# When the decay matrices of the gated delta heads are made, and in which tiles

## The chip, the cores and the metric

One core of a Trainium2 chip. The metric is the device time of one execution in microseconds (us); runs of one kernel are compared by their median. TensorE (PE) does the matrix products, VectorE (DVE), ScalarE (ACT) and GpSimd (POOL) the elementwise work, and SyncE (SP) issues most of the DMAs. PE's granted clock is shown as a share of full speed: 1.00 is 2.4 GHz, 0.50 is 1.2 GHz.

## What is computed

One decoder layer over 1024 tokens of width 2048, in float32: a modulated input is projected by one large matrix, four retention heads and eight gated delta heads mix along the sequence, an output projection and a layer norm follow. The change is in the gated delta heads. For one head, with queries q, keys k, values v (1024 x 128 each), log decays g and step sizes beta, in chunks of C tokens (64 in the reference, 128 in the kernel; the result is the same function):

```
gcum  = cumsum(g within the chunk)
decay = exp(gcum_i - gcum_j) for i >= j, else 0
A     = strictly_lower((k * beta) @ k.T * decay)
T     = inverse(I + A)
attn  = lower(q @ k.T * decay)
per chunk, with the state S carried on:
  v_new = T @ (v*beta) - T @ (k*beta*exp(gcum)) @ S
  o     = (q * exp(gcum)) @ S + attn @ v_new
  S     = S * exp(g_last) + (k * exp(g_last - gcum)).T @ v_new
```

So `decay`, a 128 x 128 matrix per chunk and head, is used twice: for A, with the keys alone, and for attn, with the queries. exp(gcum) as a row over the chunk scales the queries.

## The kernel before

**Stages.** First the modulation and the first projection columns (to about 220 us of the span), then the main stage: for each of the eight gated delta heads four projections (K, V, Q and the gate GG) of 1024 tokens by 128 columns, then three retention heads' projections, then the output projection with the layer norm (from about 1585 us). A projection (`gemm_cm`, L476) is 96 matmuls of 512 columns, each operand split in a high and a low part.

**Order.** PE's instructions run in the order in which the program writes them. Between two matmuls of a projection, `tick` (L419) lets a generator go on by one step: first one of the list `aux`, then the first of `heads`, if its waiting time, counted in ticks, has run out. So the small matmuls of the heads are woven in between the large ones at fixed places, and a `yield n` says after how many ticks the next step may come. All other engines are ordered by the framework's planner: it estimates when the inputs and the tile buffer of an operation are ready, so that an operation can stand on its engine ahead of others that were written before it. Once planned, every engine works through its list in order.

**A head** has four generators, in this order: `gdn_keys` (L759: transposes of k, the squares for its norm, k k' times decay, then a forward substitution on DVE by way of two DMA round trips through DRAM), `gdn_values` (L883), `gdn_merge` (L831: block inverses joined on PE, L850 to L880, after transposes on DVE, L840) and `gdn_scan` (L895). The merge is due 210 ticks after the end of the key step. The scan takes two halves of four chunks; before them, for each half, it makes q k' (L907), multiplies it by the decay matrix into the tile `et` (L908), transposes q (L913), sums its squares on ACT (L745) and scales q on POOL (L917). Then, chunk by chunk, with four ticks between: L930 (k times state), w on DVE (L932), L936 (inverse times w), u on ACT (L938), L942 (state update; new state on DVE, L945 or L947), L951 and L952 (output). `gdn_out` follows by way of `aux`.

**The decay matrix.** `decay_prep` stores gcum of all chunks and heads in DRAM (`gc_d`, L718). `gate_rows` (L736) loads one half of a head, 4 chunks x 128, to all 128 partitions (256 KB) into a tile of the tag `gb` with two buffers; the tag is also used by `gdn_merge` (Tm) and by the loads of the modulation gate in the later stage (graw). `decay_matrix` (L751) adds the column term and the mask on DVE (four L755 of 128 x 128) and takes the exponential on ACT (L757, 128 x 512). `gdn_keys` does this in place in gb for both halves, `gdn_scan` does it again into et, takes the exponential of the row itself (L915) and multiplies q by it (L917). That makes four loads, 16 L755, four L757 and two L915 per head.

Of the kernel before, what the change touches and what calls it, by code (L numbers as in the profile page):

```python
# [7 lines left out]
F32 = mybir.dt.float32  # L8
F32R = mybir.dt.float32r
I32 = mybir.dt.int32  # L10
AF = mybir.ActivationFunctionType
ALU = mybir.AluOpType
# [3 lines left out]
P = 128  # L16
# [6 lines left out]
GH = 8  # L23
# [35 lines left out]
def hybrid_layer_kernel(ctx: ExitStack, tc: tile.TileContext, x, c, w_ada, b_ada, w_in, gdn_conv_w,  # L59
                        gdn_a_log, gdn_dt_bias, ret_gn_w, ret_gn_b, gdn_norm_w, w_out, ln_w, ln_b,  # L60
                        tab, out):
    nc = tc.nc
# [350 lines left out]
    def spawn(gen, wait=0.0):  # L413
        heads.append([gen, clock[0] + wait])
# [260 lines left out]
    def decay_prep(gab, dec):  # L675
        n = [P, NC, GH]
        ones_ = mp.tile([P, P], F32, name="ones_", tag="gb", bufs=2)
        V.memset(ones_, 1.0)
        tmpt = mp.tile([P, 4, NC, GH], F32, name="dtmp", tag="ktok")

        def tl(nm):
            return const.tile(n, F32, name=nm, tag=nm)
        alog = const.tile([P, GH], F32, name="alog")
        dtb = const.tile([P, GH], F32, name="dtb")
        nc.sync.dma_start(out=alog, in_=gdn_a_log.broadcast_to([P, GH]))
        nc.sync.dma_start(out=dtb, in_=gdn_dt_bias.broadcast_to([P, GH]))
        S.activation(out=alog, in_=alog, func=AF.Exp)
        ga, e, z, z2 = (tmpt[:, i] for i in range(4))
        g = tl("g_")
        V.tensor_tensor(out=ga, in0=gab[:, :, 0:8], in1=dtb[:, None, :].broadcast_to(n), op=ALU.add)  # L690
        V.scalar_tensor_tensor(out=e, in0=ga, scalar=-1.0, in1=ga, op0=ALU.mult, op1=ALU.max)
        S.activation(out=e, in_=e, func=AF.Exp, scale=-1.0)
        V.tensor_scalar(out=z, in0=e, scalar1=2.0, scalar2=None, op0=ALU.add)
        V.reciprocal(out=z, in_=z)
        V.tensor_tensor(out=z, in0=z, in1=e, op=ALU.mult)
        V.tensor_tensor(out=z2, in0=z, in1=z, op=ALU.mult)
        V.tensor_scalar(out=g, in0=z2, scalar1=1.0 / 15, scalar2=None, op0=ALU.mult)
        for d in (13, 11, 9, 7, 5, 3):
            V.scalar_tensor_tensor(out=g, in0=g, scalar=1.0 / d, in1=z2, op0=ALU.add, op1=ALU.mult)
        V.scalar_tensor_tensor(out=g, in0=g, scalar=1.0, in1=z, op0=ALU.add, op1=ALU.mult)  # L700
        V.tensor_scalar(out=ga, in0=ga, scalar1=0.0, scalar2=None, op0=ALU.max)
        V.scalar_tensor_tensor(out=g, in0=g, scalar=2.0, in1=ga, op0=ALU.mult, op1=ALU.add)
        V.scalar_tensor_tensor(out=g, in0=g, scalar=-1.0, in1=alog[:, None, :].broadcast_to(n),
                               op0=ALU.mult, op1=ALU.mult)
        beta = tl("beta")
        V.tensor_scalar(out=beta, in0=gab[:, :, 8:16], scalar1=-87.0, scalar2=None, op0=ALU.max)
        S.activation(out=beta, in_=beta, func=AF.Exp, scale=-1.0)
        V.tensor_scalar(out=beta, in0=beta, scalar1=1.0, scalar2=None, op0=ALU.add)
        V.reciprocal(out=beta, in_=beta)
        gf = g.rearrange("p c h -> p (c h)")  # L710
        yield 40
        pc = small_ps()
        PE.matmul(pc[:, 0:64], tri, gf, start=True, stop=True)
        PE.matmul(pc[:, 64:128], ones_, gf, start=True, stop=True)
        PE.matmul(pc[:64, 128:256], gf, tri, start=True, stop=True)
        gcT = mp.tile([64, P], F32, name="gcT", tag="et")
        S.copy(gcT, pc[:64, 128:256])
        nc.sync.dma_start(out=gc_d, in_=gcT)  # L718
        ngc, neg, ktl, egl = tl("ngc"), tl("neg"), tl("ktl"), tl("egl")
        pv = pc[:, 0:128].rearrange("p (a c h) -> p a c h", a=2, h=GH)  # L720
        V.tensor_scalar(out=ngc, in0=pv[:, 0], scalar1=-1.0, scalar2=None, op0=ALU.mult)
        S.activation(out=neg, in_=ngc, func=AF.Exp, scale=-1.0)
        V.tensor_scalar(out=neg, in0=neg, scalar1=-1.0, scalar2=None, op0=ALU.mult)
        S.activation(out=egl, in_=pv[:, 1], func=AF.Exp)
        V.tensor_tensor(out=ktl, in0=pv[:, 1], in1=ngc, op=ALU.add)
        S.activation(out=ktl, in_=ktl, func=AF.Exp)
        dec.update(beta=beta, ngc=ngc, neg=neg, ktl=ktl, egl=egl)
        yield 0

    B8 = [P, NC, P]  # L730
    B4 = [P, 4, P]

    def c4(t):
        return t.rearrange("p (c i) -> p c i", i=P)

    def gate_rows(h, hf):  # L736
        gb = mp.tile([P, 512], F32, name="gb", tag="gb", bufs=2)
        nc.sync.dma_start(out=c4(gb), in_=gc_d.rearrange("(c h) i -> h c i", h=GH)
                          [h:h + 1, 4 * hf:4 * hf + 4].broadcast_to(B4))
        return gb  # L740

    def sum_squares(src, dst):
        junk = gp.tile([P, P], F32, name="junk", tag="xt")
# [7 lines left out]
    def decay_matrix(h, hf, out, gb, dec):  # L751
        for j in range(4):
            ch = 4 * hf + j
            cl = slice(j * P, (j + 1) * P)
            V.scalar_tensor_tensor(out=out[:, cl], in0=gb[:, cl], scalar=dec["ngc"][:, ch, h:h + 1], in1=maske,  # L755
                                   op0=ALU.add, op1=ALU.add)
        S.activation(out=out, in_=out, func=AF.Exp)  # L757

    def gdn_keys(h, st, k, dec, Pm):  # L759
# [2 lines left out]
        nb = c4(sup[:, 1024:2048])  # L762
        kt_ = mp.tile(B8, F32, name="ktok", tag="ktok")
        ss = gp.tile([P, NC], F32, name="ssk", tag="ssk")
        ets = []
        for hf in range(2):
            gb = gate_rows(h, hf)
            decay_matrix(h, hf, gb, gb, dec)
            ets.append(c4(gb))
        for hf in range(2):  # L770
            pk = small_ps()
            for j in range(4):
# [16 lines left out]
        for hf in range(2):  # L789
            pkk = small_ps()  # L790
            for j in range(4):
                cl = slice((4 * hf + j) * P, (4 * hf + j + 1) * P)
                PE.matmul(pkk[:, j * P:(j + 1) * P], k[:, cl], k[:, cl], start=True, stop=True)  # L793
            for j in range(4):
                ch = 4 * hf + j
                V.scalar_tensor_tensor(out=nb[:, ch], in0=pkk[:, j * P:(j + 1) * P], scalar=nco[:, ch:ch + 1],
                                       in1=ets[hf][:, j], op0=ALU.mult, op1=ALU.mult)
            yield 2

        s1 = drs.tile([4, NC, 1024], F32, name="s1", tag="s1")  # L800
# [79 lines left out]
            V.tensor_copy(Pm[h0, c4s, h1], px2[h0, :, 0:64])  # L880
        yield 5

    def gdn_values(st, v):  # L883
        vs = mp.tile(B8, F32, name="vs", tag="vs")
        for hf in range(2):
            c4s = slice(4 * hf, 4 * hf + 4)
            pv = small_ps()
            for j in range(4):
                ch = 4 * hf + j
                PE.transpose(pv[:, j * P:(j + 1) * P], v[:, ch * P:(ch + 1) * P], ident)  # L890
            V.tensor_tensor(out=vs[:, c4s], in0=c4(pv), in1=st["sk"][:, c4s, None].broadcast_to(B4), op=ALU.mult)
            yield 3
        st["vs"] = vs

    def gdn_scan(h, st, k, q, dec, Pm):  # L895
        kt_, vs, co = st["kt"], st["vs"], st["co"]
        et = mp.tile(B8, F32, name="et", tag="et")
        ssq = gp.tile([P, NC], F32, name="ssq", tag="ssq")
        for hf in range(2):
            c4s = slice(4 * hf, 4 * hf + 4)  # L900
            gb = gate_rows(h, hf)
            ef = et[:, c4s].rearrange("p c i -> p (c i)")
            decay_matrix(h, hf, ef, gb, dec)
            pqk = small_ps()
            for j in range(4):
                cl = slice((4 * hf + j) * P, (4 * hf + j + 1) * P)
                PE.matmul(pqk[:, j * P:(j + 1) * P], k[:, cl], q[:, cl], start=True, stop=True)  # L907
            V.tensor_tensor(out=et[:, c4s], in0=c4(pqk), in1=et[:, c4s], op=ALU.mult)  # L908
            yield 2
            pq = small_ps()  # L910
            for j in range(4):
                ch = 4 * hf + j
                PE.transpose(pq[:, j * P:(j + 1) * P], q[:, ch * P:(ch + 1) * P], ident)  # L913
            sum_squares(pq, ssq[:, c4s])
            S.activation(out=gb, in_=gb, func=AF.Exp)  # L915
            hs = slice(hf * 512, (hf + 1) * 512)
            G.tensor_tensor(out=q[:, hs], in0=q[:, hs], in1=gb, op=ALU.mult)  # L917
            yield 2
        state = None
        for hf in range(2):  # L920
            o = mp.tile(B4, F32, name="og", tag="o", bufs=2)
# [81 lines left out]
    for h in range(GH):  # L1003
        k = conv_silu(gemm_cm(GK + h * P), 8 + h) if h else k_first
        st = {}
        spawn(gdn_keys(h, st, k, dec, Pm), CONV_WAIT if h else 0)
        v = conv_silu(gemm_cm(GV + h * P), 16 + h)
        spawn(gdn_values(st, v), 56)
        spawn(gdn_merge(st, Pm))
        q = conv_silu(gemm_cm(GQ + h * P), h)  # L1010
        spawn(gdn_scan(h, st, k, q, dec, Pm), 38)
        st["sg"] = silu_gate(gemm_cm(GG + h * P))
# [237 lines left out]
```

## Time and profile before

| what | value |
|---|---|
| median of 3 runs | 1962.99 us (1962.37 to 1963.16) |
| the profiled execution | 1964.96 us, its span 1963.20 us |
| PE busy | 1875.3 us, 96% of the span |
| DVE, ACT, POOL busy | 58%, 28%, 9% |
| mean granted clock | 0.988 |
| stage of the gated delta heads | about 220 to 1160 us of the span |

Busy time of PE is that of its matmuls; their ends are modelled, since matmuls overlap. In a row of the timeline the first number is the start in us of the span, the second the time from start to end of what the row merges, `x2` the number of instructions, and in brackets stands how long the engine was idle just before and what ended that. One product of 32-bit operands is two instructions in the small matmuls.

### The profile page before, as it was taken

The numbers are of one execution on the slowest core, as the hardware profiler recorded it, in microseconds if no ns is written. First come the engines' busy times: TensorE is split into PE (matmuls) and PEld (weight loads), VectorE is DVE, ScalarE is ACT, GpSimd is POOL, SyncE is SP. The second block draws the span as 40 slices with busy tenths as digits, with TensorE's granted clock in tenths as the row PEclk, the third lists the DMA queues.
The fourth block names the chain that finished last, engine by engine and source line by source line (L and its number), as shares of the span: only waits on it lengthen the run. The fifth ranks groups of instructions, "written<-read, shape, count | busy, mean of one in ns | idle before, by whom it ended". The sixth has DMA issues, their size and how long they took to land.

```text
span 1963.2 us, 27906 instructions
## 1 busy us (share of the span) xinstructions
PE 1875.3 (96%) x10336; PEld 1584.3 (81%) x10336; DVE 1143.9 (58%) x2833; ACT 555.0 (28%) x1243; POOL 170.4 (9%) x165
## 2 busy tenths in 40 slices
PE   4999999999999999999999999999999999998996
PEld 3788878787878788787878798898898878886885
DVE  6785666575746657574756642544542534458557
ACT  2543232323223231423223221211211232234221
POOL 0000111000000000100000000100100100005102
PEclk9999999999999999999999999999999999999998
DMA  9994223221222212221222241144141266345532
GB/s 293 324 305 133 72 50 84 49 72 45 77 51 73 54 55 67 54 73 49 68 56 72 65 124 49 49 140 134 44 129 48 65 202 227 124 135 185 180 115 89
DMA packets 249195, 210.07 MB, mean 107 GB/s; under 512 B 44425, under 2 KB 208858, under 8 KB 248290
## 3 DMA queue, kind: packets, MB, share of 16 engines
q1 hardware_dynamic: 246434, 199.89, 34.7%
q0 software_dynamic: 2624, 8.39, 1.2%
q8 instruction: 81, 1.33, 0.3%
q14 instruction: 56, 0.46, 0.1%
HBM read 189.31 MB, written 18.92 MB: 106 GB/s over the span
## 4 chain that ended last, share of the span: by engine, by line
PE 72%; DMA 6%; DVE 4%; issue 1%; POOL 1%; ACT 1%; SPq 0%; DVEq 0%; ACTq 0%; POOLq 0%
PE pg L476 44%; PE po L1105 14%; PE pg L508 6%; DMA gb<-gc_d 4%; DMA raw<-mixed 1%; DMA graw<-in_w_ada_dram 1%; PE ps L793 1%; POOL z L1161 1%; PE ps L936 1%; PE ps L930 1%; DVE et L755 1%; PE ps L952 1%; PE ps L603 1%; PE ps L951 1%; POOL yc L917 0%
## 5 line engine op out<-in xcount | busy, mean ns | idle before, releaser
L476 PE MATMUL pg<-h_hi,w_hi 128*128 128x512 f32 x1376 | 451.7, 400 | 0.0
L476 PE MATMUL pg<-h_hi,w_lo 128*128 128x512 f32 x1376 | 448.5, 399 | 0.0
L476 PE MATMUL pg<-h_lo,w_hi 128*128 128x512 f32 x1376 | 447.4, 399 | 0.0
L1105 PE MATMUL po<-wr,ms 128*128 128x512 f32 x1380 | 319.6, 393 | 8.4 <-DVE wr L1052 5.8
L1105 PEld LDWEIGHTS po<-wr,ms 128*128 128x128 f32 x1380 | 260.9, 190 | 65.4 <-DVE wr L1052 8.1
L94 ACT CAST w_hi<-w_raw 128x512 fp32r<-128x512 f32 (+1 forms) x203 | 126.1, 621 | 603.8 <-PE pg L476 455.3
L476 PEld LDWEIGHTS pg<-h_hi,w_hi 128*128 128x128 f32 x1376 | 256.4, 189 | 48.9 <-ACT w_hi L94 1.7
L476 PEld LDWEIGHTS pg<-h_lo,w_hi 128*128 128x128 f32 x1376 | 257.3, 189 | 47.6
L476 PEld LDWEIGHTS pg<-h_hi,w_lo 128*128 128x128 f32 x1376 | 256.7, 188 | 47.5 <-issue 0.2
L95 DVE TENSOR_TENSOR w_lo<-w_raw,w_hi 128x512 fp32r<-128x512 f32 (+1 forms) x203 | 144.6, 712 | 218.9 <-ACT w_hi L94 214.5
L1052 DVE TENSOR_TENSOR wr<-raw,wr 128x512 fp32r<-128x512 f32 x116 | 88.1, 762 | 109.9 <-ACT wr L1050 107.9
L508 PE MATMUL pg<-w_lo,h_hi 128*128 128x256 f32 (+1 forms) x448 | 128.7, 287 | 3.4 <-DVE w_lo L95 3.4
L508 PE MATMUL pg<-w_hi,h_hi 128*128 128x256 f32 (+1 forms) x448 | 129.1, 288 | 1.4 <-DVE part L324 1.4
L508 PE MATMUL pg<-w_hi,h_lo 128*128 128x256 f32 (+1 forms) x448 | 128.9, 288 | 0.0
L1050 ACT CAST wr<-raw 128x512 fp32r<-128x512 f32 x116 | 71.6, 621 | 157.0 <-PE po L1105 148.4
L666 DVE SCALAR_TENSOR_TENSOR yc<-pg,cw,yc 128x1023 f32<-128x1023 f32 (+2 forms) x69 | 88.3, 1279 | 2.9 <-ACT yc L663 1.9
L508 PEld LDWEIGHTS pg<-w_lo,h_hi 128*128 128x128 f32 x448 | 86.3, 193 | 3.9 <-DVE w_lo L95 3.8
L508 PEld LDWEIGHTS pg<-w_hi,h_hi 128*128 128x128 f32 x448 | 86.4, 193 | 3.5 <-ACT w_hi L94 1.7
L508 PEld LDWEIGHTS pg<-w_hi,h_lo 128*128 128x128 f32 x448 | 86.4, 193 | 0.0
L208 DVE SCALAR_TENSOR_TENSOR acc<-wa,cs,acc 128x512 f32<-128x512 f32 x104 | 73.3, 746 | 5.5 <-DMA wa<-in_w_ada_dram 5.1
L456 DVE SCALAR_TENSOR_TENSOR gacc<-graw,cs,gacc 128x512 f32<-128x512 f32 x60 | 49.2, 821 | 45.8 <-DMA graw<-in_w_ada_dram 45.2
L307 PE MATMUL pg<-h_hi,w_hi 128*128 128x512 f32 x160 | 55.1, 427 | 7.9 <-ACT h_hi L242 7.9
(253 smaller groups left out, 2355.3 us busy)
## 6 DMA issues: line engine op xcount, KB each, us to landing
w_raw<-in_w_in_dram SPq DMA_DIRECT2D x204, 256.0 KB
wa<-in_w_ada_dram SPq DMA_DIRECT2D x128, 256.0 KB
raw<-in_w_out_dram SPq DMA_DIRECT2D x128, 256.0 KB
graw<-in_w_ada_dram SPq DMA_DIRECT2D x64, 256.0 KB
xs<-in_x_dram SPq DMA_DIRECT2D x16, 512.0 KB
gb<-gc_d SPq DMA_DIRECT2D x32, 256.0 KB
raw<-mixed SPq DMA_DIRECT2D x32, 256.0 KB
z<-in_x_dram SPq DMA_DIRECT2D x32, 256.0 KB
```

The costliest lines, as they stand in the source:

```text
L94: S.copy(hi[:, :n], raw[:, :n])
L95: V.tensor_tensor(out=lo[:, :n], in0=raw[:, :n], in1=hi[:, :n].bitcast(F32), op=ALU.subtract)
L208: V.scalar_tensor_tensor(out=a, in0=wr, scalar=cs[:, r:r + 1], in1=zero.broadcast_to([P, 4 * P]) if r < 2 else a, op0=ALU.mult, op1=ALU.add)
L307: PE.matmul(ps0[t][:, i * 512:(i + 1) * 512], w[:, t * P:(t + 1) * P], hh[:, i * 512:(i + 1) * 512], start=(first and w is hi and hh is hH ...
L456: V.scalar_tensor_tensor(out=a, in0=raw[:, :512], scalar=cs[:, r:r + 1], in1=a, op0=ALU.mult, op1=ALU.add)
L476: PE.matmul(pt[:, i * 512:(i + 1) * 512], w[:, kk], hh[:, i * 512:(i + 1) * 512], start=(kt == 0 and w is hi and hh is hH[kt]), stop=(kt = ...
L508: PE.matmul(dsts[tt - tts[0]], hh[:, tsl], w[:, kk], start=(kt == 0 and first_in_bank and hh is hH[kt] and w is hi), stop=(kt == KT - 1 an ...
L603: PE.matmul(po[:, :DV], sc[:, ch], vt[:, ch], start=(ch == 0), stop=True)
L666: V.scalar_tensor_tensor(out=y[:, s:], in0=pt[:, :T - s], scalar=cw[:, j * 24 + ti:j * 24 + ti + 1], in1=y[:, s:], op0=ALU.mult, op1=ALU.add)
L1050: S.copy(t[:, :512], raw)
L1052: V.tensor_tensor(out=t[:, 512:], in0=raw, in1=t[:, :512].bitcast(F32), op=ALU.subtract)
L1105: PE.matmul(pts[tt], m[:, a + tt * P:a + (tt + 1) * P], w, start=(n == 0 and a == 0 and w is wh), stop=(n == KT - 1 and a == 512))
```

## The change

The two halves of a head's rows get a tag of their own, `gr`, with four buffers in the pool `gdnp`. `gate_load(h)` loads them; it is called at the end of `decay_prep` for head 0 and in the key step of head h for head h+1. `gate_decay(h)` makes both halves of the decay matrix in one tile et (of the pool `gdnp` for even heads, `mp` for odd ones) and takes the exponential of the rows in place; it is called in the key step for head 0 and at the end of the value step of head h for head h+1. The key step and the scan read what is there; the scan multiplies q k' into the same et. The second half of the scan's preparation yields 8 ticks instead of 2.

```diff
@@ decay_prep
         dec.update(beta=beta, ngc=ngc, neg=neg, ktl=ktl, egl=egl)
+        gate_load(0)
         yield 0
@@
-    def gate_rows(h, hf):
-        gb = mp.tile([P, 512], F32, name="gb", tag="gb", bufs=2)
-        nc.sync.dma_start(out=c4(gb), in_=gc_d.rearrange("(c h) i -> h c i", h=GH)
-                          [h:h + 1, 4 * hf:4 * hf + 4].broadcast_to(B4))
-        return gb
+    gates = {}
+
+    def gate_load(h):
+        if h >= GH:
+            return
+        gates[h] = []
+        for hf in range(2):
+            gr = gp.tile([P, 512], F32, name="gr", tag="gr", bufs=4)
+            nc.sync.dma_start(out=c4(gr), in_=gc_d.rearrange("(c h) i -> h c i", h=GH)
+                              [h:h + 1, 4 * hf:4 * hf + 4].broadcast_to(B4))
+            gates[h].append(gr)
+
+    def gate_decay(h, dec):
+        if h >= GH:
+            return
+        et = (mp if h % 2 else gp).tile(B8, F32, name="et", tag="et")
+        for hf in range(2):
+            decay_matrix(h, hf, et[:, 4 * hf:4 * hf + 4].rearrange("p c i -> p (c i)"), gates[h][hf], dec)
+        for gr in gates[h]:
+            S.activation(out=gr, in_=gr, func=AF.Exp)
+        gates[h].append(et)
@@ gdn_keys
-        ets = []
-        for hf in range(2):
-            gb = gate_rows(h, hf)
-            decay_matrix(h, hf, gb, gb, dec)
-            ets.append(c4(gb))
+        if h == 0:
+            gate_decay(0, dec)
+        et = gates[h][2]
+        gate_load(h + 1)
...
-                                       in1=ets[hf][:, j], op0=ALU.mult, op1=ALU.mult)
+                                       in1=et[:, ch], op0=ALU.mult, op1=ALU.mult)
@@ gdn_values
-    def gdn_values(st, v):
+    def gdn_values(h, st, v, dec):
...
         st["vs"] = vs
+        gate_decay(h + 1, dec)
@@ gdn_scan
-        et = mp.tile(B8, F32, name="et", tag="et")
+        *rows, et = gates.pop(h)
...
-            gb = gate_rows(h, hf)
-            ef = et[:, c4s].rearrange("p c i -> p (c i)")
-            decay_matrix(h, hf, ef, gb, dec)
...
-            S.activation(out=gb, in_=gb, func=AF.Exp)
             hs = slice(hf * 512, (hf + 1) * 512)
-            G.tensor_tensor(out=q[:, hs], in0=q[:, hs], in1=gb, op=ALU.mult)
-            yield 2
+            G.tensor_tensor(out=q[:, hs], in0=q[:, hs], in1=rows[hf], op=ALU.mult)
+            yield 2 + 6 * hf
```

## Rows read from the trace of the kernel before

**Rows 1.** The page: busy time, share of the span and instructions of each engine.
```profile
PE 1875.3 (96%) x10336; PEld 1584.3 (81%) x10336; DVE 1143.9 (58%) x2833; ACT 555.0 (28%) x1243; POOL 170.4 (9%) x165
```
**Rows 2.** The page: the chain that ended last, its shares by line.
```profile
PE pg L476 44%; PE po L1105 14%; PE pg L508 6%; DMA gb<-gc_d 4%; DMA raw<-mixed 1%; DMA graw<-in_w_ada_dram 1%; PE ps L793 1%; POOL z L1161 1%; PE ps L936 1%; PE ps L930 1%; DVE et L755 1%; PE ps L952 1%; PE ps L603 1%; PE ps L951 1%; POOL yc L917 0%
```
**Rows 3.** Waits of PE: waiting line, releaser: us in total, times, longest.
```profile
PE ps L942 <- ACT u L938: 10.6, 8, 2.5
...
PE ps L936 <- DVE w L932: 6.8, 8, 1.8
...
PE ps L930 <- DVE gs L947: 4.2, 6, 1.0
PE ps L930 <- DVE gs L945: 2.9, 2, 2.5
```
**Rows 4.** Timeline of PE, scan of head 3: its three waits.
```profile
678.10 0.49 PE L942 MATMUL ps<-u,ktok 128*128 128x128 f32 x2 [1.04 <-ACT u L938]
...
681.40 0.46 PE L936 MATMUL ps<-w,Pm 128*128 128x128 f32 x2 [0.51 <-DVE w L932]
...
685.15 0.49 PE L930 MATMUL ps<-gs,yc 128*128 128x128 f32 x2 [0.76 <-DVE gs L947]
```
**Rows 5.** Timeline of ACT, the same scan.
```profile
673.58 0.63 ACT L757 ACTIVATE et<-et 128x512 f32<-128x512 f32 x1 [11.40 <-DVE et L755]
...
677.66 0.39 ACT L938 ACTIVATE u<-ps,co 128x128 f32<-128x128 f32 x1
```
**Rows 6.** Timeline of DVE, the same scan.
```profile
683.70 1.14 DVE L755 SCALAR_TENSOR_TENSOR gb<-gb,ngc,maske 128x128 f32<-128x128 f32 x4 [2.44 <-DMA gb<-gc_d]
```
**Rows 7.** Timeline of SP's queue, the same scan.
```profile
677.39 0.36 SPq L738 DMA_DIRECT2D gb<-gc_d  x1
```
**Rows 8.** Groups of DVE by line: count, busy us, mean ns, idle before.
```profile
L666 DVE SCALAR_TENSOR_TENSOR yc<-pg,cw,yc 128x1023 f32<-128x1023 f32 (+2 forms) x69 | 88.3, 1279 | 2.9 <-ACT yc L663 1.9
...
L755 DVE SCALAR_TENSOR_TENSOR et<-gb,ngc,maske 128x128 f32<-128x128 f32 x64 | 23.3, 395 | 17.1 <-DMA gb<-gc_d 17.1
```
**Rows 9.** Timeline of DVE and of PE, head 5: last transposes, first merge product.
```profile
875.84 2.60 DVE L840 STREAM_TRANSPOSE Tm<-Pm 32x32 f32<-32x32 f32 x24
...
884.53 0.36 PE L850 MATMUL ps<-Tm,sup 32*32 32x32 f32 x6
```
**Rows 10.** Timeline of PE, head 5: behind a wait, and in flow.
```profile
902.13 0.49 PE L942 MATMUL ps<-u,ktok 128*128 128x128 f32 x2 [2.44 <-ACT u L938]
902.46 0.39 PE L952 MATMUL ps<-u,et 128*128 128x128 f32 x2
...
905.68 0.40 PE L476 MATMUL pg<-h_hi,w_hi 128*128 128x512 f32 x1
905.92 0.38 PE L942 MATMUL ps<-u,ktok 128*128 128x128 f32 x2
906.14 0.39 PE L951 MATMUL ps<-gs,yc 128*128 128x128 f32 x2
```
**Rows 11.** Timeline of PE: waits of head 0 and of head 7.
```profile
359.28 0.49 PE L930 MATMUL ps<-gs,yc 128*128 128x128 f32 x2 [2.49 <-DVE gs L945]
...
1125.62 0.80 PE L942 MATMUL ps<-u,ktok 128*128 128x128 f32 x2 [2.46 <-ACT u L938]
...
1156.61 0.49 PE L936 MATMUL ps<-w,Pm 128*128 128x128 f32 x2 [0.72 <-DVE w L932]
```
**Rows 12.** Stretches: us, busy (instructions) of PE, PEld, DVE, ACT, POOL; PEclk, DMA, GB/s.
```profile
360.00:368.00 8.00, 6.62 (x23) 5.40 (x22) 4.74 (x10) 3.22 (x9) 0.00 (x0) 0.57 0.16 40
1126.00:1130.00 4.00, 4.00 (x25) 4.00 (x24) 1.95 (x5) 1.12 (x7) 0.00 (x0) 0.62 0.50 159
...
902.00:908.00 6.00, 5.54 (x30) 4.49 (x30) 3.40 (x12) 2.50 (x12) 0.00 (x0) 1.00 0.29 83
```
**Rows 13.** Timeline of PE and of ACT, head 5's last product and the next convolution.
```profile
931.05 0.39 PE L952 MATMUL ps<-u,et 128*128 128x128 f32 x2
...
932.70 1.11 ACT L663 ACTIVATE yc<-pg,cw 128x1024 f32<-128x1024 f32 x1
```

More of the change, by code (lines that the diff above doesn't have):

```diff
@@ L1007, in hybrid_layer_kernel @@
         v = conv_silu(gemm_cm(GV + h * P), 16 + h)
-        spawn(gdn_values(st, v), 56)
+        spawn(gdn_values(h, st, v, dec), 56)
         spawn(gdn_merge(st, Pm))
```

## The prediction, made before the changed kernel ran

> **What bounds the kernel.** I read the summary first: TensorE (PE) is busy 96% of the span [rows 1], and the change leaves every matrix instruction in place. So it can gain only where PE stands still or runs slowly. The chain of waits comes next: after the three projection lines its largest item is a transfer, gb<-gc_d, 4% of the span [rows 2]. This is the load of the decay rows that the change moves. The chain follows one order of releases, though, so its 78 us are not PE time; what PE lost is in its own waits. Four groups stand out, all in the scan of the gated delta heads: L942 for u (10.6 us), L936 for w (6.8), L930 for the state (4.2 and 2.9) [rows 3]. That is 24.5 us in 24 waits. The other PE waits of the kernel belong to other stages, and stay.
>
> Head 3 shows the pattern of the heads [rows 4]: three waits early in the scan and none in the later chunks, though these run the same instructions.
> - The first u. ScalarE (ACT) sat 11.40 us idle until the scan's own et was ready, then ran two exponentials for the decay and the row, and the squares of q behind them; u of chunk 0 came 4.08 us after the first of them [rows 5]. PE had come to L942 1.04 us earlier.
> - w of chunk 1 and the state of chunk 2. VectorE (DVE) stood before decay_matrix of the *next* head's keys, whose rows were still on their way: before the state, 2.44 us of waiting and 1.14 us of work [rows 6], before w the same with a shorter wait. The second load was issued at 677.39, when a buffer of the tag gb came free, and its data was used at 683.70: 6.3 us [rows 6, 7]. So that work is written after the scan and runs inside it, as soon as its buffer allows.
>
> **The change, part by part, per head.**
> - Scan: two loads, eight L755, two L757 and two L915 leave it. L915 isn't removed, it moves to gate_decay. Removed for good are 64 L755 of 0.40 us (23.3 us of DVE) [rows 8], 16 L757 of 0.63 us (10 us of ACT) [rows 5] and 16 of 32 loads. None of that is PE time; alone it is worth nothing.
> - Keys: decays and loads of the head's own rows leave it too (but for head 0), so what stood inside the scan of the head before goes. gate_load(h+1) puts two loads there. With four buffers, gr of h+1 needs only the release by the q multiplication of head h-1, a scan earlier; the planner can issue the load in that scan, and nothing there waits for it. SP then sees two issues per head (0.36 us each [rows 7]) where it saw four; weight loads queue behind fewer loads that wait for a buffer.
> - Values: gate_decay(h+1), eight L755 (2.8 to 3.2 us) and four exponentials (2.5 us). et alternates between two pools, so et of h+1 is free when the scan of h-1 has read it last; the work can't stand inside that scan, and it is written before the scan of h. In between lie the key work and the solve. If all of it fell into the solve, it would add at most 3.2 us to a chain that has 6.1 us to spare: the transposes end at 878.44, and PE starts the merge that reads them at 884.53 [rows 9]. I cost it at nothing; without that cover it is 3.2 us a head.
> - The yield of 8 instead of 2 holds chunk 0 for six more matmul ticks of 0.23 us [rows 10], 1.4 us in which PE works on the projection. It removes no PE work and adds none; it delays the scan's last chunk by 1.4 us against the gemm.
> - POOL keeps its 16 products; they read gr in place of gb. Head 0 loads its rows after the same store as before, with head 1's two loads behind them (0.7 us of SP): nothing. The larger gdnp pool (four gr of 2 KB and an et of 4 KB per partition) can reach into the space of the later rotary table; its load would then wait for the last head, with a whole projection before its use: nothing.
>
> **The sum.** Three of the 24 waits, 1.5 us, come in head 7 from the modulation gate's accumulation (the longest is in [rows 11]); I leave them. The other 21 are 23.0 us. Each costs more than its idle time. A flowing L942 starts 0.24 us after the matmul ahead, whose modelled duration is 0.40 us, so some 0.16 us before each wait is not shown as idle; and behind the wait the next group starts 0.33 us later instead of 0.22 [rows 10]. That is 0.27 us, 5.7 us for 21. Third, the clock. In head 0 the wait of 2.49 us [rows 11] is followed by a stretch of 8 us with a granted clock of 0.57, in head 7 a wait of 2.46 us by 4 us at 0.62 [rows 11, 12]: the lower level, 1.2 GHz, for part of each. Busy time times the lost share is 6.62 x 0.43 + 4.00 x 0.38 = 4.4 us. Together 33.1 us.
>
> Against it stands what may stay. The first u: without two exponentials (1.2 us) and with 1.4 us more, the wait of 1.04 us has 1.6 us to spare, and that of 2.44 us in head 5 [rows 10] has 0.2 us. ACT can also do the first squares while it idled. A new wait costs between nothing (as in the later chunks) and all that head 3 loses, 2.31 us a head. I take a third of the u wait, 0.35 us, since the ACT queue is what is left in front of chunk 0: 2.8 us for eight heads. **The gain is 30.3 us.** The profiled execution took 1964.96 us (span 1963.20 and 1.76 around it), 1.97 us above the median of 1962.99; it becomes 1934.7, and the median 1932.7.
>
> On the clock: head 5's wait of 2.44 us [rows 10] left the clock at 1.00 [rows 12], head 7's of 2.46 did not, so a wait of this size doesn't always cost it. The Trainium skill, "TensorE: Matmul & The Clock Gate", section "HAM oscillation — how this bites in real kernels", says that idle stretches between bursts put the array back to half rate. By that, closing the gaps also removes both slow stretches, as in my sum; were they independent of the gaps, the sum would be 25.9 us and the time 1937.1.
>
> **The rivals.**
> - *Half of it.* The DMA and DVE waits go but the first u stays, because the squares of q, the gate's tanh and the weight casts still fill ACT. For: these stood between the exponentials and u. Against: ACT's idle 11.40 us. It keeps 10.6 + 8 x 0.27 = 12.8 us: a gain of 17.5 us, 1945.5. Chance 0.14.
> - *Nothing moves where it counts.* The planner orders DVE and ACT itself and could put the decays of h+1 back into a scan, waiting there as now. For: it did so with the keys' decays. Against: et frees only at a scan's end. No gain, 1963, within 4 us. Chance 0.06.
> - *Slower: the last chunk meets the next convolution.* Head 5's scan ends with L952 at 931.05, and the convolution of the next keys starts on ACT at 932.70 for 1.11 us, with three L666 of 1.28 us behind it on DVE [rows 8, 13]. The delay of 1.4 us takes most of the 1.65 us between. If the planner put chunk 7's w behind the three L666, PE would wait 3.8 us in seven heads, 28.8 us with the restarts, and with a slow stretch like head 0's (2.85 us) each time 48.7 us: 18 us slower than before, 1981. It decides once the delay passes about 3 us; 1.4 us is half of that. Chance 0.05.
>
> **How the numbers follow.** My forecast has 0.75, from 1926 (all 33.1 us and a few more from waits that I left) to 1939. The range is 1925 to 1948: the forecast and the better half of the first rival. A measurement here tells 0.2%, about 4 us, from no change. Faster by more than that are the forecast and the first rival, 0.89; within it 0.06; slower 0.05.
>
> **What would show it.** After the change the chain of waits has no gc_d load worth naming, PE's waits for L942, L936 and L930 add up to under 5 us, no L755 stands between a scan's first L936 and its last, and the clock is 1.00 in every scan. The first step is wrong if L942 still waits for u after the squares; the second if gr loads end waits on DVE inside a scan; the cover is gone if PE waits at L850 for the transposes; and the last rival shows as PE waits just before the next keys' convolution. A gain under 15 us makes the forecast wrong.

## The result, and the profile after

The changed kernel took 1939.78 us (median of 4 runs, 1936.34 to 1943.95), the kernel before 1963.08 us on the same chip (4 runs, 1962.37 to 1965.62). The ratio is 0.9882, 95% interval 0.9868 to 0.9896: 23.3 us faster, between 20.4 and 25.9 us. The forecast was 1932.7 us in a range of 1925 to 1948. So the sign and the mechanism held, and 30.3 us of gain was 7 us too much: 1939.78 us lies in the range, but above the 1926 to 1939 that the prediction gave its forecast.

The profiled execution took 1942.35 us, with a span of 1940.6 us. Of the 22.6 us by which its span is shorter, PE's idle time gave 17.6 (87.9 to 70.3 us) and PE's busy time 5.0 (1875.3 to 1870.3). Lines have moved in the program: L930, L936 and L942 of before are L945, L951 and L957 now, L755 is L774, L840 and L850 are L858 and L868, L976 is L991, and L738 is L746.

The page of the changed kernel, busy time of each engine, and its chain by line [rows 1, 2]:

```profile
PE 1870.3 (96%) x10336; PEld 1584.5 (82%) x10336; DVE 1119.6 (58%) x2769; ACT 546.1 (28%) x1227; POOL 165.9 (9%) x165
...
PE pg L476 45%; PE po L1120 15%; PE pg L508 7%; DVE yc L666 1%; PE ps L923 1%; PE ps L951 1%; PE ps L967 1%; PE ps L957 1%; PE ps L811 1%; PE ps L945 1%; PE ps L966 1%; POOL z L1176 1%; PE ps L603 1%; PE ps L889 0%; PE ps L896 0%
```

DVE lost 64 instructions and 24.3 us, and the load of the gate rows, 4% of the chain before, is no longer in it. The scan's own lines, in the view that groups PE's instructions by line (count, busy us, mean ns, idle before):

```profile
L957 PE MATMUL ps<-u,ktok 128*128 128x128 f32 x112 | 22.1, 279 | 0.0
L951 PE MATMUL ps<-w,Pm 128*128 128x128 f32 x112 | 21.8, 276 | 0.1
L945 PE MATMUL ps<-gs,yc 128*128 128x128 f32 x112 | 21.6, 275 | 0.4 <-DVE gs L962 0.4
```

Of the 24.5 us of [rows 3], 0.4 us is left. Also gone are the three waits of head 7 that the forecast had left in place. What PE waits for in the delta heads now, in the view of its waits (us in total, times, longest):

```profile
PE ps L991 <- POOL og L985: 2.9, 3, 1.2
...
PE ps L908 <- DVE sup L814: 1.2, 1, 1.2
PE ps L868 <- DVE Tm L858: 0.9, 1, 0.9
```

L908 is the old L890, which waited 0.3 us; the other two are new. The sum of the idle time closes: 24.1 us less in the scans, 2.9, 0.9 and 0.9 us more here, 1.1 us more before the output projection (L1120, 6.9 us against 5.8), and some 0.3 us more in other waits, give 18.0 us against the 17.6 measured.

**The first u.** ACT's timeline of head 3's scan, where [rows 5] had 11.40 us of idle time before the first exponential:

```profile
666.59 0.28 ACT L764 ACTIVATE junk<-ps 128x128 f32<-128x128 f32 x1 [11.04 <-PE ps L929]
...
670.93 0.37 ACT L953 ACTIVATE u<-ps,co 128x128 f32<-128x128 f32 x1
```

The squares of q now begin as soon as PE has made the transposes, with no exponential ahead of them, and u of chunk 0 follows 4.34 us after the first of them. PE does not wait for it.

**The output behind the scan.** DVE's timeline of head 3's scan end, and behind it the lines of POOL and of PE that follow from it:

```profile
700.01 0.61 DVE L774 SCALAR_TENSOR_TENSOR et<-gr,ngc,maske 128x128 f32<-128x128 f32 x2
700.54 1.28 DVE L666 SCALAR_TENSOR_TENSOR yc<-pg,cw,yc 128x1023 f32<-128x1023 f32 x1
701.73 0.15 DVE L983 SCALAR_TENSOR_TENSOR xo<-so,xo 128x4 f32<-128x4 f32 x1
701.80 0.35 DVE L774 SCALAR_TENSOR_TENSOR et<-gr,ngc,maske 128x128 f32<-128x128 f32 x1
...
708.89 0.16 DVE L119 SCALAR_TENSOR_TENSOR f<-rs_o,f 128x4 f32<-128x4 f32 x1
```
```profile
709.21 1.03 POOL L985 TENSOR_TENSOR og<-og,f 128x512 f32<-128x512 f32 x1 [9.72 <-ACT gr L758]
```
```profile
710.30 0.66 PE L991 MATMUL ps<-ident,og 128*128 128x128 f32 x4 [1.16 <-POOL og L985]
```

These L774 are the eight decay products of head 5, which takes the tile et of head 3. They come the moment it is free, at the end of this scan (its last L967 starts at 699.44), ahead of the key work of head 4, behind which the program writes them. They share DVE with the next convolution (three L666) and with the small instructions that scale this scan's output (L983 to L119). The output's factor f is ready at 709.05, POOL's product at 710.24, and PE waits 1.16 us for it. (The bracket of POOL's line names an exponential on ACT that ended about then; but the product starts 0.14 to 0.18 us behind f in all 16 cases, here 0.16, so f is what it waits for.)

**Head 1's merge and the clock.** DVE's transposes for head 1's merge, and PE's first merge products (what [rows 9] shows for head 5 of the kernel before):

```profile
440.40 2.60 DVE L858 STREAM_TRANSPOSE Tm<-Pm 32x32 f32<-32x32 f32 x24 [1.78 <-DMA Pm<-s]
```
```profile
441.03 0.43 PE L868 MATMUL ps<-Tm,sup 32*32 32x32 f32 x8
442.41 0.90 PE L868 MATMUL ps<-Tm,sup 32*32 32x32 f32 x24 [0.94 <-DVE Tm L858]
```

PE does not come sooner. From head 1's last key products (L793 before, L811 now) to its first merge product it takes 50.51 us in both kernels. It is the solve that takes longer: the transposes end 49.3 us behind the key products before, and 52.5 us now. The loss arises at the start of the solve, in the eight products of k k' with the decay matrix (L796, now L814). The kernel before, on PE and on DVE:

```profile
395.79 1.05 PE L793 MATMUL ps<-yc 128*128 128x128 f32 x8
...
446.30 0.89 PE L850 MATMUL ps<-Tm,sup 32*32 32x32 f32 x32
```
```profile
401.02 2.15 DVE L796 SCALAR_TENSOR_TENSOR sup<-ps,nco,gb 128x128 f32<-128x128 f32 x8
...
443.70 1.36 DVE L840 STREAM_TRANSPOSE Tm<-Pm 32x32 f32<-32x32 f32 x12
```

The changed kernel:

```profile
390.52 1.05 PE L811 MATMUL ps<-yc 128*128 128x128 f32 x8
```
```profile
394.88 1.28 DVE L666 SCALAR_TENSOR_TENSOR yc<-pg,cw,yc 128x1021 f32<-128x1021 f32 x1
...
398.18 0.68 DVE L672 SCALAR_TENSOR_TENSOR yc<-th,yc 128x512 f32<-128x512 f32 x1
...
403.37 0.35 DVE L814 SCALAR_TENSOR_TENSOR sup<-ps,nco,et 128x128 f32<-128x128 f32 x1
```

All three L666 and both L672 of a convolution now stand ahead of these products (the last of each is shown), where one L666 did. So the eight products end 13.2 us behind the key products instead of 7.4; later steps win back 2.6 us. Why the planner orders DVE so is not shown.

The stretches of [rows 12] and the one that follows this wait (us, busy of PE, PEld, DVE, ACT, POOL, then the granted clock):

```profile
360.00:368.00 8.00, 7.96 (x45) 6.35 (x44) 5.80 (x10) 3.30 (x11) 0.00 (x0) 1.00 0.16 43
444.00:457.00 13.00, 13.00 (x97) 10.05 (x96) 4.38 (x12) 0.00 (x0) 0.52 (x1) 0.51 0.08 21
1126.00:1130.00 4.00, 4.00 (x37) 4.00 (x36) 1.30 (x3) 1.57 (x6) 0.00 (x0) 1.00 0.01 2
```

Both slow stretches of [rows 12] run at 1.00 now, 2.4 GHz. A new one has come: 13 us at 0.51, the lower level of 1.2 GHz, which costs 13.00 x 0.49 = 6.4 us. In the kernel before, 444 to 457 us had a granted clock of 1.00. Two of the four runs were near 1937 us with a mean granted clock of 0.992 over the run, two near 1943 us with 0.987 and 0.989, the profiled one among them. The gap of 6 us is the size of this stretch.

### The profile page after: what moved, and what is told of

It reads as the page before. It is cut to its first block, busy times and chain, and to the rows that moved or that the text cites. A ratio compares the mean times of both kernels' runs of the same rounds, so it can differ in the third digit from the quotient of the medians.

```text
span 1940.6 us, 27794 instructions
## 1 busy us (share of the span) xinstructions
PE 1870.3 (96%) x10336; PEld 1584.5 (82%) x10336; DVE 1119.6 (58%) x2769; ACT 546.1 (28%) x1227; POOL 165.9 (9%) x165
## 4 chain that ended last, share of the span: by engine, by line
PE 77%; DVE 5%; issue 1%; POOL 1%; DMA 0%; ACT 0%; SPq 0%; POOLq 0%; DVEq 0%; ACTq 0%
PE pg L476 45%; PE po L1120 15%; PE pg L508 7%; DVE yc L666 1%; PE ps L923 1%; PE ps L951 1%; PE ps L967 1%; PE ps L957 1%; PE ps L811 1%; PE ps L945 1%; PE ps L966 1%; POOL z L1176 1%; PE ps L603 1%; PE ps L889 0%; PE ps L896 0%
## 5 line engine op out<-in xcount | busy, mean ns | idle before, releaser
L1120 PE MATMUL po<-wr,ms 128*128 128x512 f32 x1380 | 318.0, 392 | 9.5 <-DVE wr L1067 6.9
L1120 PEld LDWEIGHTS po<-wr,ms 128*128 128x128 f32 x1380 | 260.3, 189 | 65.4 <-DVE wr L1067 8.5
L1067 DVE TENSOR_TENSOR wr<-raw,wr 128x512 fp32r<-128x512 f32 x116 | 87.9, 762 | 110.6 <-ACT wr L1065 106.5
L666 DVE SCALAR_TENSOR_TENSOR yc<-pg,cw,yc 128x1023 f32<-128x1023 f32 (+2 forms) x69 | 88.3, 1279 | 4.3 <-ACT yc L663 3.0
```

The costliest lines, as they stand in the source:

```text
L666: V.scalar_tensor_tensor(out=y[:, s:], in0=pt[:, :T - s], scalar=cw[:, j * 24 + ti:j * 24 + ti + 1], in1=y[:, s:], op0=ALU.mult, op1=ALU.add)
L1067: V.tensor_tensor(out=t[:, 512:], in0=raw, in1=t[:, :512].bitcast(F32), op=ALU.subtract)
L1120: PE.matmul(pts[tt], m[:, a + tt * P:a + (tt + 1) * P], w, start=(n == 0 and a == 0 and w is wh), stop=(n == KT - 1 and a == 512))
```

## The experiments

Two questions: which part of the change brought the gain, and what took the missing 7 us. Every kernel ran in several rounds against the kernel before, whose median was 1963.19, 1964.53 and 1964.19 us in the three batches.

### What brought the gain

**Only the six ticks, on the kernel before** (e2_ticks_only).

```
-            yield 2
+            yield 2 + 6 * hf
```


> The kernel before with nothing but the six ticks in front of chunk 0. Theory: the waits behind the next head's rows (w 6.8 and states 7.1 us) stay, and of the 10.6 us for u most go; 1.4 us of PE work per head covers the shorter ones: 1963 minus 7 to 12, so 1951 to 1956. Rival (the ticks carry the gain): 1940 or less. Second rival (the ticks only shift the waits, and scans run into the next convolution): 1960 or more.

Measured: 1982.35 us (1975.11 to 1991.27), ratio 1.0100 (1.0078 to 1.0121): 19 us slower. The theory's 1951 to 1956 us did not come; the time is the second rival's. Its waits of PE, SP's queue and ACT's timeline in head 0's scan:

```profile
PE ps L942 <- ACT u L938: 13.8, 7, 3.7
PE ps L930 <- DVE gs L945: 7.3, 5, 3.7
```
```profile
353.91 2.58 SPq L738 DMA_DIRECT2D gb<-gc_d  x2
```
```profile
360.46 0.63 ACT L757 ACTIVATE gb<-gb 128x512 f32<-128x512 f32 x1 [3.48 <-DVE gb L755]
360.99 0.35 ACT L938 ACTIVATE u<-ps,co 128x128 f32<-128x128 f32 x1
```

The delay lets the planner put the *next* head's decay (L757 on gb) ahead of this head's u, and its rows had been asked for only at 353.91. ACT stands 3.48 us for them, and u stands behind. More room in the program did not help while the load was late; it let more late work in. These waits are not all of the loss. Of the 17.5 us by which the profiled span is longer than before's, 7.9 are PE's idle time and 9.6 its busy time, which goes with new slow stretches. The longest is 448 to 468 us, at 0.57, behind 1.6 us of waits at head 1's merge.

**Only four tiles for the rows, on the kernel before** (e9_four_tiles). No load, matrix or tick is moved.

```
-        gb = mp.tile([P, 512], F32, name="gb", tag="gb", bufs=2)
+        gb = gp.tile([P, 512], F32, name="gb", tag="gr", bufs=4)
```


> The kernel before with one edit: the gate rows get four tiles of their own in place of the two that they share with the chunk merge's Tm. No load, matrix or tick is moved in the program; a load may start as soon as its tile is free. Theory (the loads came late because their two tiles were still in use, and early loads are most of the gain): the scan's PE waits fall from 24.5 us to under 6 us, time 1937 to 1946 us. Rival (the place of issue decides, so the loads must be written a head ahead): the waits stay above 15 us, 1955 to 1964 us.

Measured: 1949.08 us (1947.08 to 1951.94), ratio 0.9924 (0.9908 to 0.9941): 15 us of the 23. Its waits of PE, and DVE's decay products by line:

```profile
PE ps L976 <- POOL og L970: 5.1, 5, 1.0
...
PE ps L850 <- DVE Tm L840: 2.8, 2, 1.6
...
PE ps L942 <- ACT u L938: 0.4, 1, 0.4
```
```profile
L755 DVE SCALAR_TENSOR_TENSOR et<-gb,ngc,maske 128x128 f32<-128x128 f32 x64 | 20.8, 347 | 10.0 <-PE ps L952 10.0
L755 DVE SCALAR_TENSOR_TENSOR gb<-gb,ngc,maske 128x128 f32<-128x128 f32 x64 | 20.2, 346 | 30.9 <-DMA gb<-gc_d 30.9
```

The scan's waits fall from 24.5 to 0.4 us, although every matrix is still made twice. The theory on the waits is shown; the time is 3 us above its range. The waits for the output (5.1 us) and for the merge (2.8 us) are 4.1 us longer than in the changed kernel. Both waits for the merge (1.55 and 1.23 us) are head 1's, though no work was moved. The second fence says why the scan is free: its own products (et<-gb) no longer wait for a transfer but for the end of the scan before. With free tiles the loads are issued earlier by themselves: the last of the 32 at 1003.2 us of the span, before at 1113.7. The keys' products still wait for theirs, 30.9 us of DVE time, but not inside a scan. What the loads themselves waited for, in SP's queue, first in the kernel before and then with four tiles:

```profile
SPq L738 <- POOL yc L917: 48.4, 13, 6.6
SPq L738 <- PE ps L871: 34.9, 8, 7.8
```
```profile
SPq L738 <- POOL yc L917: 67.1, 14, 10.7
SPq L738 <- DVE sup L796: 28.4, 6, 7.1
```

Eight times, 34.9 us in all, a load stood in the queue until L871, the merge's product that reads Tm, had given a tile back. That wait is gone.

**Rows loaded a head ahead, matrices still made twice** (e5_loads_only).

```
-        if h == 0:
-            gate_decay(0, dec)
-        et = gates[h][2]
+        et = []
+        for hf in range(2):
+            gb = mp.tile([P, 512], F32, name="gb", tag="gb", bufs=2)
+            decay_matrix(h, hf, gb, gates[h][hf], dec)
+            et.append(c4(gb))
...
-        gate_decay(h + 1, dec)
...
+            decay_matrix(h, hf, et[:, c4s].rearrange("p c i -> p (c i)"), rows[hf], dec)
```


> Only the loads move: the gate rows have four tiles of their own and are loaded a head ahead, as in the changed kernel, but each decay matrix is made twice again, in the chunk stage of its own head and again at the start of its scan; the six ticks stay. Theory (the 23 us come from the rows arriving late, since the two executions in which the scan waited stood behind a load that had just been issued): the scan's PE waits stay under 6 us in sum, time 1936 to 1946 us. Rival (they come from the second making of the matrices, eight VectorE products of 0.33 us and two exponentials of 0.63 us ahead of u): 16 makings cost 0.7 us of wait each, about 11 us, time 1948 to 1954 us.

Measured: 1942.80 us (1938.97 to 1943.46), ratio 0.9887 (0.9871 to 0.9902): the changed kernel's time, within the interval. PE waits 0.3 us in its scans. The theory is shown: making the matrices once, which saves 64 products and 16 exponentials, is worth nothing that can be measured here. Against four tiles alone (1949.08 us, 0.9908 to 0.9941) it is 6 us faster; the loads written ahead and the six ticks are what it has more.

**Made once, but in the chunk stage of its own head and in one tile** (e6_same_head).

```
-        et = (mp if h % 2 else gp).tile(B8, F32, name="et", tag="et")
+        et = mp.tile(B8, F32, name="et", tag="et")
...
-        if h == 0:
-            gate_decay(0, dec)
+        gate_decay(h, dec)
...
-        gate_decay(h + 1, dec)
```


> Rows loaded a head ahead and each matrix made once, but in the chunk stage of its own head and in one tile instead of two. Theory (loading early and making once is enough): time 1934 to 1944 us, and the 2.9 us at L991, where the next head's eight products stood between the scan's end and its output, go. Rival (the matrix must be a head ahead and in two tiles: with one tile the next head's products wait until the scan has read the last of the old one, and the chunk products behind them wait too): 2 to 3 us of PE wait in each of seven heads, time 1952 to 1960 us.

Measured: 1945.14 us (1939.05 to 1945.89), ratio 0.9896 (0.9880 to 0.9913): at most a little slower than the changed kernel, its interval overlapping. Its waits of PE:

```profile
PE ps L989 <- POOL og L983: 3.4, 4, 1.2
...
PE ps L907 <- DVE sup L813: 2.9, 1, 2.9
```

Its time is 1 us above the theory's range and far below the rival's. Neither side had it whole. The 2 to 3 us per head of the rival are not there; but the wait for the output does not go either (3.4 us, theory said none), and a wait of 2.9 us stands in the first head, before L907. So a head ahead and two tiles bring at most these few microseconds.

### What took the missing part

**The changed kernel without the six ticks** (e1_no_ticks).

```
-            yield 2 + 6 * hf
+            yield 2
```


> The changed kernel with the old yield of 2 ticks in both halves. Theory (what was taken out of the scan carries the gain, the six ticks are a margin): the wait of L957 (the state update, L942 before) for the first u comes back only where it was longest, in heads 5 and 7, where it was 2.44 and 2.46 us and two exponentials of 0.6 us have gone: about 1.2 us each, 2.5 us in all. The waits of L991 for the output's scaling (2.9 us after the change) go, since each scan ends 1.4 us sooner. So within 4 us of the changed kernel, 1936 to 1944. Rival (the six ticks carry it): the u waits come back as they were, 10 us and their restarts, 1952 or more.

Measured: 1946.06 us (1945.60 to 1949.05), ratio 0.9917 (0.9903 to 0.9931), 2 us above the theory's range. Its waits of PE, and the stretch behind head 1's merge:

```profile
PE ps L991 <- POOL og L985: 3.9, 4, 1.0
...
PE ps L868 <- DVE Tm L858: 1.8, 1, 1.8
...
PE ps L957 <- ACT u L953: 0.4, 1, 0.4
```
```profile
444.00:457.00 13.00, 13.00 (x99) 10.03 (x98) 4.67 (x14) 0.62 (x1) 0.52 (x1) 0.53 0.08 21
```

The ticks neither hold off a wait for u (0.4 us without them) nor cause the waits for the output (3.9 us without them). What differs is head 1's merge: its wait is 1.8 us instead of 0.9, and all six runs have a mean granted clock of 0.987 to 0.989. PE again takes 50.5 us from the key products to the merge; the transposes end 53.3 us behind them.

**The merge due 8 ticks later** (e3_merge_later).

```
-    BASE_WAIT = 210
+    BASE_WAIT = 218
```


> The changed kernel with the merge due 218 instead of 210 ticks after the key step, 1.8 us later. Theory (PE, no longer waiting in the scan, now reaches head 1's merge 0.94 us ahead of its transposes, and this wait ahead of many small matmuls sets off the slow clock of 444 to 457 us, about 7 us in the runs at 1942 and 1944): no wait at L868, clock 1.00 from 430 to 470 us, and all runs near the lower group, 1933 to 1938, within 3 us of each other. Rival (the slow clock comes of the small matmuls or of chance, not of the wait): the runs still fall into two groups some 6 us apart.

Measured: 1935.51 us (1934.56 to 1936.02), ratio 0.9860 (0.9845 to 0.9875). All four runs have 0.991 or 0.992, so the time no longer falls into two groups. The first merge products on PE's timeline, and the two stretches around them:

```profile
446.17 0.89 PE L868 MATMUL ps<-Tm,sup 32*32 32x32 f32 x32
```
```profile
440.00:450.00 10.00, 10.00 (x115) 8.06 (x114) 5.68 (x34) 0.62 (x1) 0.54 (x2) 1.00 0.29 67
450.00:460.00 10.00, 9.91 (x77) 8.15 (x77) 4.51 (x11) 2.14 (x10) 1.86 (x3) 1.00 0.10 28
```

The 32 products run without a wait and the clock stays at 1.00. PE now takes 52.3 us from head 1's key products to the merge, and the transposes end at 51.6. The waits for the output have gone as well; three waits for w, 1.6 us in all, are new. The interval touches that of the changed kernel (0.9868 to 0.9896), so the 4 us between them rest on more than this run: with the next two kernels that have the later merge (e8, e7), 12 runs lie between 1934.11 and 1938.39 us, where the changed kernel's four reach 1943.95.

**Later merge and no ticks** (e8_no_ticks_later): the two edits above together.

> The changed kernel without the six ticks, with the merge due 8 ticks later (218). Theory (the ticks act on the time by where head 1's merge lands, and by nothing else): as the later merge with the ticks, 1934.5 to 1937 us, no wait for Tm at L868 and no half clock at 440 to 460 us. Rival (the ticks are worth what the run without them lost, whatever the merge does): 1941 to 1944 us.

Measured: 1935.74 us (1934.11 to 1936.35), ratio 0.9854 (0.9840 to 0.9868). PE does not wait at L868, and no stretch of 10 us between 200 and 1160 us is below 1.00. So what the ticks are worth goes with head 1's merge: nothing of it is left once the merge is due later. Against e1, the same kernel with the merge at 210, it is 10 us, and the intervals are far apart.

**The output's scaling ahead of other work** (e4_out_first): the four statements that make f and og stand under `with tc.high_priority():`.

> The changed kernel with the output's scaling (two DVE instructions, the reciprocal root and the POOL product of gdn_out) put ahead of other work in the planner. Theory (the decays now stand at the scan's end, between the convolution and that root, and hold the output's transposes up by 1.2, 0.5 and 1.2 us in heads 3 to 5): no wait at L991, 3 to 4 us less in each group of runs. Rival (the product on POOL is late for another reason, or PE loses elsewhere what it gains): no difference beyond 1.5 us.

Measured: 1937.29 us (1936.28 to 1939.84), ratio 0.9871 (0.9856 to 0.9887); the wait for the output falls from 2.9 to 1.3 us. The interval overlaps the changed kernel's, so neither the theory's 3 to 4 us nor the rival's nothing is shown. The wait at head 1's merge stayed, 1.1 us, and yet the stretch behind it, in this profiled run, was not slow:

```profile
444.00:457.00 13.00, 13.00 (x132) 10.87 (x132) 6.57 (x16) 3.13 (x15) 2.90 (x3) 1.00 0.11 28
```

So a wait of about 1 us there is followed by the lower clock in some runs, and not in others.

**Both** (e7_both_fixes): later merge and output first.

> The merge due 8 ticks later (218) and the output's scaling ahead of other work, together. Theory (the later merge already moved the next head's products away from the output, so the second edit finds nothing to do): 1935.5 us, within 1 us of the later merge alone. Rival (the two are separate losses and add up): 1932 to 1933.5 us.

Measured: 1936.29 us (1935.20 to 1938.39), ratio 0.9860 (0.9843 to 0.9877): as the later merge alone. PE waits for no output in either, so the second edit had nothing to do.

**The later merge on the kernel before** (e10_before_later).

> The kernel before with the merge due 8 ticks later (218) and nothing else. Theory (the later merge only undoes a loss that the change brought, the wait at head 1's merge and the half clock behind it, which before did not have): no change, 1960 to 1966 us. Rival (it is worth the same 4 us on either kernel): 1958 to 1960 us.

Measured: 1975.20 us (1971.86 to 1976.86), ratio 1.0055 (1.0037 to 1.0073): 11 us *slower*, which neither side expected. A wait of PE that was not there before, and what the loads waited for in SP's queue:

```profile
PE ps L936 <- DVE et L908: 3.9, 5, 0.9
```
```profile
SPq L738 <- PE ps L871: 39.9, 7, 6.3
...
SPq L738 <- DVE vv L873: 7.3, 1, 7.3
```

The loads wait 47.2 us for the merge in place of 34.9: it comes later and holds the tiles longer, and five times the scan's first chunk now waits for the scan's own matrices. Their waits for L917 fall at the same time, from 48.4 to 31.7 us, so that all their waits together are only some 3 us longer. That this is all of the 11 us is not shown.

**Four tiles and the later merge, on the kernel before** (e11_tiles_later): these two one-line edits alone.

> The two edits of the other runs of this call together: four tiles, merge due at 218. Theory (early loads are most of the gain, the rest is where head 1's merge lands): 1933 to 1938 us, no wait for Tm in the merge. Rival (making the matrices once, a head ahead, is worth something of its own, which only the whole change has): 1939 to 1945 us.

Measured: 1941.12 us (1938.33 to 1946.50), ratio 0.9887 (0.9867 to 0.9906). With the tiles apart, the later merge takes 8 us off (1949.08 to 1941.12), where with shared tiles it added 11. Against the whole change with the later merge (1935.51 us) 5.6 us are missing, as the rival said. PE's waits for the output (2.4 us) and for the merge (1.0, where the theory had none) are not there in e3; that for w (2.0) is much the same. Three of the six runs are near 1939 us at a mean granted clock of 0.991 to 0.993, three at 1943 to 1946.5 with 0.987 to 0.990, so part of the 5.6 us goes with the clock. Which of the loads written ahead, the single making and the two tiles gives the rest was not tried with the merge at 218; it is not the ticks, as e8 without them is as fast.

The fastest kernels are the changed one with the merge due at 218, with or without the ticks: 1935.5 and 1935.7 us, 4 us under the change as it stands.

## Why the prediction was right, point by point

- *What bounds the kernel*: right. The gain came from the scan's PE waits, and the load behind them was the reason. The prediction saw that the load was issued "when a buffer of the tag gb came free" [rows 6, 7], and named the four buffers, but valued the change by what it moves, and gave the tiles no worth of their own. By e9 the four tiles alone free the scan.
- *Removed work is worth nothing by itself*: right, by e5.
- *23.0 us of waits*: right, and a little low. 24.1 us went, head 7's three waits with the rest; why those went was not tried.
- *2.8 us for new waits at the first u*: not needed. With the squares running as soon as the transposes are there, u met PE in every scan of the changed kernel, and without the ticks all but once (0.4 us). The reason given for the six ticks fell too, by e1 and e8.
- *Restarts, 5.7 us*: not isolated, but of the right size. From the kernel before to e3, which has no slow stretch at the merge, PE's busy time falls by 1875.3 - 1865.1 = 10.2 us; the two slow stretches account for 4.4, and 5.8 are left. Some 1.3 of these belong to the output stage, where a slow stretch is milder in e3 (1764 to 1776 us: 7.60 us busy at 0.86; before, 1792 to 1804 us: 8.47 at 0.72).
- *The clock, 4.4 us*: the two stretches went as forecast, 0.57 and 0.62 to 1.00. The Trainium skill's rule, "TensorE: Matmul & The Clock Gate", section "HAM oscillation — how this bites in real kernels", that idle stretches put the array back to half rate, agrees with that: with the waits the slow stretches went. Not every wait had brought one, as head 5's of 2.44 us shows [rows 10, 12]. The term that failed is that nothing takes their place: 6.4 us came back in head 1.
- *The values step at nothing*: **this step failed twice.** First, the cover. I took 6.1 us of spare time from head 5 [rows 9] for all heads. Heads 3 to 7 have it in the changed kernel too (6.1 to 6.4 us). But in the kernel before, head 1's last transpose ended at 445.06 and its first product began at 446.30, so 1.24 us were spare there, and in head 0 only 0.71. The sign "the cover is gone if PE waits at L850 for the transposes" came true in head 1. The moved work does not stand in what used the cover up: no L774 is in head 1's solve, and with four tiles alone (e9), where the program moves nothing, PE waits longer at the same place. What used it up is the order of DVE at the start of the solve, which made the solve 3.2 us longer; what the planner took this order from is not shown. Second, the place. "et of h+1 is free when the scan of h-1 has read it last" was right, and the planner put the products there at once, ahead of the key work: on the stretch where DVE scales that scan's output. That goes with 2.9 us in three heads, a term I didn't have; e4, which puts the scaling ahead, leaves 1.3 of them. By e3, e7 and e8 the wait at the merge and the clock behind it are some 4 us of the median.
- *The six ticks*: "delays the scan's last chunk by 1.4 us", with no new wait there, was right: in head 3, chunk 0 begins 2.30 us behind q's second transposes, and 0.91 us without the ticks (e1). The rival "last chunk meets the next convolution" did not occur; of its place, DVE behind the scan, the output felt something, the chunks did not.
- *The rivals "half of it" and "nothing moves where it counts"* did not occur: the first u does not wait, and no L774 stands in a scan. The sum of the first takes the 2.8 us off twice: 33.1 - 12.8 is a gain of 20.3 us, 1942.7 instead of 1945.5.

From forecast to profiled run 30.3 - 22.6 = 7.7 us are missing. The slow stretch (6.4), the output (2.9), the merge (0.9), L908 (0.9) and other waits (1.4) are 12.5 us of it; the reserve for u (2.8), head 7 (1.1), and a stretch at 220 to 230 us, 0.83 before and 1.00 now (1.7), give back 5.6. That is 6.9 of 7.7, with the restarts taken as forecast. So errors on both sides partly cancel. And the measured time lies in the part of the range that the prediction took from its first rival, whose mechanism did not occur: that the range held is in part luck.

## What to carry to other kernels

When a wait ends with a load, ask first what held the load's tile: who else uses those buffers, and when that user is done. Here one line that gave the rows tiles of their own brought 15 of 23 us, while a delay that only made room, or a later due time, made the kernel 19 and 11 us slower as long as the tiles were shared. And cover for moved work has to be measured in every head that it moves into, since the tightest one decides, and measured again after the change: the planner ordered DVE anew, and head 1's solve took 3.2 us longer though no work was moved into it.

## What the runs showed of the hardware

A wait of about 1 us before the merge's small products was followed by TensorE's lower level in one profiled run (0.94 us, then 13 us at 0.51), and not in another kernel's (1.1 us, granted clock 1.00). Over all 13 profiled runs: with no wait at head 1's merge the clock behind it stayed at 1.00 in all five (before, e3, e7, e8, e10). With waits of 0.9 to 2.8 us in sum it fell in five of eight (0.50 to 0.59 in the changed kernel, e1, e2, e5 and e9; 1.00 in e4, e6 and e11, whose waits were 1.1, 1.2 and 1.0 us). Runs of the same program differ as well: 1936.34 us at a mean clock of 0.992, and 1943.95 at 0.987. So a wait of 0.9 us could go with a loss of 7 us; what decided it in a given run stays open.
